# Low-part subtractions and mask additions on VectorE instead of GpSimd, in a one-layer conv and mLSTM kernel

## The chip, the cores and the metric

The kernel runs on one core of a Trainium2 chip. The metric is the device time of one execution in microseconds (us); the number given is the median of three runs. A profile is one execution recorded by the hardware, with its own span. Engine names in it: PE is TensorE (PEld its weight loads), DVE is VectorE, ACT is ScalarE, POOL is GpSimd, SP is SyncE, which here issues the DMAs.

## What is computed

One layer, applied to 128 context tokens and 2048 latent tokens of width 1024. The mixer joins a gated short convolution (512 channels) with a bidirectional mLSTM (4 heads of 128, chunks of 128 tokens); then comes a gated up projection with a convolution of width 3 over rows of the token grid, and a down projection. Everything is float32.

```python
def trunk_layer(x, mod, row_len, ffn_axis, C0, n0, m0, ...):
    shift1, scale1, gate1, shift2, scale2, gate2 = jnp.split(mod, 6, axis=-1)
    h = rmsnorm(x, norm1) * (1 + scale1) + shift1
    z = h @ w_in
    sc_b, sc_c, sc_x, q, k, v, o, g = jnp.split(z, idx, axis=-1)
    y_sc = sc_b * conv3(sc_c * sc_x, conv_sc_w, conv_sc_b)
    h_m, C, n, m = mlstm_bidir(q, k, v, gates(g), C0, n0, m0)   # chunked scans, forward and backward
    h_m = h_m * lax.rsqrt(jnp.mean(h_m * h_m, axis=-1, keepdims=True) + EPS) * mh_norm * jax.nn.sigmoid(o)
    x = x + gate1 * (jnp.concatenate([y_sc, h_m], axis=-1) @ w_out)
    h2 = rmsnorm(x, norm2) * (1 + scale2) + shift2
    a, gg = jnp.split(conv3(h2 @ w_up, conv_ffn_w, conv_ffn_b), 2, axis=-1)
    return x + gate2 * ((jax.nn.silu(gg) * a) @ w_down), C, n, m
```

Shapes, reshapes and biases are cut. `w_in` is 1024 x 3600, `w_up` 1024 x 5632, `w_down` 2816 x 1024. The outputs are the normed tokens of both groups and the final states of the context.

## The kernel before

**Products.** Each float32 product is three matmuls in a faster 32-bit format (fp32r): both operands are split into a high part (a copy rounded to that format, on ScalarE) and a low part (the operand minus its high part), and high·high, high·low and low·high are added in PSUM. So wherever a weight or an activation is loaded there is a ScalarE copy and a subtraction, and the subtraction of the low part is what the change moves. `load_w` (lines 101 to 109) splits the mixer's weights, 1024 columns at a time in two halves (line 108); `apply` (line 181) the normed tokens, every second block of 128 channels; `weights` (line 276) those of the up projection, `load_d` (line 993) those of the down projection in pieces of 704 columns.

**Stages.** The start (0 to about 130 us) prepares the modulation and the first normed tokens. To about 490 us come value and gate projections, the keys and the short convolution; to about 690 us the *Sums* weave, which carries the gated sums of keys and values over the chunks; to about 1020 us the *Mix* weave, which computes each chunk's output; to about 1180 us the output projection's rest and the sums of the normed tokens for the second half. The up projection (1180 to 2085) uses a Strassen–Winograd scheme: seven products per pair of blocks, whose combined operands come from `sums` (tokens, line 235) and `weights`. The down projection and the final norm end the run.

**The Mix weave.** A unit is a chunk and a pair of heads, 34 in all. `weave` runs them as a software pipeline: in one pass of its loop stand `first` of unit i, `third` of unit i−3, `second` of unit i−1, `load` of unit i+1, and a block of the projections' matmuls from `fill`, in every third pass a second one. So there are n + 4 = 38 passes.

- `load` fetches keys, queries, values and R, a broadcast read of 512 KB (line 742; three buffers).
- `first` multiplies keys and queries into S (line 753), adds the mask to R (line 754), takes exponentials on ScalarE (line 758), multiplies R with the queries into qs (line 761) and with S (line 762).
- `second` multiplies into y in PSUM (lines 773 and 775; one buffer), steps the state sf (line 779), and normalises: den (lines 783 to 785), then hv from y in two pairs of a ScalarE and a VectorE instruction (lines 790 and 791). The next unit's y can begin when the second line 791 has read the last.
- `third` transposes (line 803), scales into o2 (line 805) and stores it (line 808).

The blocks between them are `heads`, `shortconv` and `out_proj`; the last splits its tokens at lines 406 and 407 and adds squares at line 441.

**Order.** The kernel is written for a framework that places each instruction itself: from the text it builds a dependency graph, estimates what each instruction costs and when its inputs are there, and issues each engine's instructions in the order that follows. An engine then runs its queue strictly in order, and SP issues the DMAs in order too. An instruction given to another engine therefore also changes what stands before and behind it there.

Of the kernel before, what the change touches and what calls it, by code (L numbers as in the profile page):

```python
# [18 lines left out]
P = 128  # L19
# [26 lines left out]


def spans(t0, t1):
    """Token spans with the conditioning that they take."""
    return [(a, b, v) for a, b, v in ((t0, min(t1, P), 0), (max(t0, P), t1, 1)) if a < b]  # L50


# [1 line left out]
def hymba_kernel(ctx: ExitStack, tc: tile.TileContext, I, O):  # L54
# [46 lines left out]
    def load_w(src, n=1024):  # L101
        st = wp.tile([P, WN], F32, name="wst", bufs=2)
        Q.dma_start(st[:, :n], src)
        wh = wp.tile([P, WN], F32R, name="wh")
        S.activation(wh[:, :n], st[:, :n], AF.Copy)  # L105
        wl = wp.tile([P, WN], F32R, name="wl")
        for a in (0, n // 2):
            G.tensor_sub(wl[:, a:a + n // 2], st[:, a:a + n // 2], wh[:, a:a + n // 2].bitcast(F32))  # L108
        return wh, wl

    def affine(n, k0, k1):
# [2 lines left out]
                               bc(nrm[:, n, k0:k1, None], [P, k1 - k0, 2]), op0=ALU.add, op1=ALU.mult)  # L114

    def inv_rms(ss, n, r):
        """r [n tokens as columns of 128] = rsqrt(mean + eps) from the partial sums ss [P, n]."""
        nch = (n + P - 1) // P
        ps = pst.tile([P, 512], F32, name="st")
        for i in range(nch):  # L120
            w = min(P, n - i * P)
            PE.matmul(ps[:w, i:i + 1], ss[:, i * P:i * P + w], ones[:, 0:1], start=True, stop=True)
        for i0, i1, w in ((0, n // P, P), (n // P, nch, n % P)):
            if i0 < i1 and w:
                V.tensor_scalar(r[:w, i0:i1], ps[:w, i0:i1], 1.0 / D, EPS, op0=ALU.mult, op1=ALU.add)
                G.tensor_tensor(r[:w, i0:i1], r[:w, i0:i1], mhalf[:w, i0:i1], op=ALU.pow)  # L126

    def spread(r, n):
        """PSUM [P, n]: the columns of r along the free dimension, on every partition."""
        ps = pst.tile([P, 512], F32, name="st")  # L130
        for i in range((n + P - 1) // P):
            w = min(P, n - i * P)
            PE.matmul(ps[:, i * P:i * P + w], bc(r[:w, i:i + 1], [w, P]), ident[:w, :w], start=True, stop=True)  # L133
        return ps
# [27 lines left out]
    def apply(b, xt, norm):  # L162
        t0, n = BL[b]
        rb = spread(rcol(b), n)
        hH, hL = h_pair()
        sh = 0 if norm == 0 else 24
        for k in range(KT):
            x = xt[k // 4][:, k % 4]
            for a, e, v in spans(t0, t0 + n):
                a, e = a - t0, e - t0  # L170
                V.scalar_tensor_tensor(x[:, a:e], x[:, a:e], ab[:, norm, k, v:v + 1], rb[:, a:e],
                                       op0=ALU.mult, op1=ALU.mult)
                sv = modT[:, sh + k, v:v + 1]
                if k % 2 == 0:
                    S.activation(hH[:, k, a:e], x[:, a:e], AF.Identity, bias=sv)
                    V.scalar_tensor_tensor(hL[:, k, a:e], x[:, a:e], sv, hH[:, k, a:e].bitcast(F32),
                                           op0=ALU.add, op1=ALU.subtract)
                else:
                    S.activation(x[:, a:e], x[:, a:e], AF.Identity, bias=sv)
                    S.activation(hH[:, k, a:e], x[:, a:e], AF.Copy)  # L180
                    G.tensor_sub(hL[:, k, a:e], x[:, a:e], hH[:, k, a:e].bitcast(F32))
        return hH, hL

    def h_pair():
# [13 lines left out]
            PE.matmul(acc[:, :n], w_l, hH[:, k, :n], start=False, stop=(k == KT - 1))  # L198
        return acc

    # ------------------------------------------------------------- FFN
    # The up projection in seven products of half size (Strassen-Winograd): of the token blocks B11 B12
    # (first half of the features) and B21 B22, and of the weights' quarters A11 A12 (of a) and A21 A22 (of g).
    # A slot of the sums of tokens holds, for two pairs of blocks, 0: B12-B11, 1: B22-B12+B11, 2: B22-B12,
    # 3: B21-(1), 4: B21, 5: B22, 6: B11.
    ORDER = (6, 0, 1, 5, 2, 4, 3)

    def sums(hf, pool, pairs=range(2), direct=()):
        """The sums of the normed tokens of a half, to DRAM."""
        for p in pairs:  # L210
            t0 = hf * NU + 2 * NB * p
            rb = pool.tile([P, 2 * NB], F32, name="rb", bufs=1)
# [7 lines left out]
            for kk in range(4):  # L220
                f = pool.tile([P, 8 * NB], F32, name="F", bufs=2)
                xs_ = [(k, f[:, i * NB:(i + 2) * NB]) for i, k in ((4, kk + 4), (6, kk))]
                for k, x in xs_:
                    Q.dma_start(x, xD[k][:, t0:t0 + 2 * NB])
                yield
                for k, x in xs_:
                    for a, e, v in spans(t0, t0 + 2 * NB):
                        a, e = a - t0, e - t0
                        V.scalar_tensor_tensor(x[:, a:e], x[:, a:e], ab[:, 1, k, v:v + 1], rb[:, a:e],
                                               op0=ALU.mult, op1=ALU.mult)  # L230
                        S.activation(x[:, a:e], x[:, a:e], AF.Identity, bias=modT[:, 24 + k, v:v + 1])
                f = f.rearrange("p (i t) -> p i t", t=NB)
                V.tensor_sub(f[:, 0], f[:, 7], f[:, 6])
                V.tensor_sub(f[:, 1], f[:, 5], f[:, 0])
                G.tensor_sub(f[:, 2], f[:, 5], f[:, 7])
                V.tensor_sub(f[:, 3], f[:, 4], f[:, 1])
                for i in direct:
                    th, tl = slots[i]
                    S.activation(th[:, 4 * p + kk], f[:, i], AF.Copy)
                    V.tensor_sub(tl[:, 4 * p + kk], f[:, i], th[:, 4 * p + kk].bitcast(F32))  # L240
                yield
                i0, i1 = int(0 in direct), 7 - int(6 in direct)
                Q.dma_start(tD[hf, i0:i1, :, 4 * p + kk].rearrange("i p t -> p i t"), f[:, i0:i1])
# [14 lines left out]
            V.tensor_sub(tl[:, q], x, th[:, q].bitcast(F32))  # L258

    def weights(j):  # L260
        """The split weights of the seven products."""
        st = fp.tile([P, 2, 1024], F32, name="st", bufs=2)
        for m in range(2):
            Q.dma_start(st[:, m], I["w_up"][m * FT + j])
# [4 lines left out]
            op(t, a, b)  # L269
            return t  # L270

        def part(a, on_pool):
            wh = fp.tile([P, 512], F32R, name="wh", bufs=3)
            wl = fp.tile([P, 512], F32R, name="wl", bufs=3)
            S.activation(wh, a, AF.Copy)  # L275
            (G if on_pool else V).tensor_sub(wl, a, wh.bitcast(F32))  # L276
            return wh, wl

        yield part(a11, True)
        s1 = add(V.tensor_add, a21, a22, "s1")  # L280
        yield part(s1, False)
        s2 = add(V.tensor_sub, s1, a11, "s2")
        yield part(s2, False)
        s4 = add(V.tensor_sub, a12, s2, "s4")
        yield part(s4, False)
        s3 = add(V.tensor_sub, a11, a21, "s3")
        yield part(s3, False)
        yield part(a12, True)
        yield part(a22, True)

    def stages():
        """Products of all units, in order, each with its weights."""
        for hf in range(2):
            for j in range(FT):
                for i, w in enumerate(weights(j)):
                    yield hf, j, i, w

    # ---------------------------------------------------------------- mixer
    ph2 = ExitStack()
    with ExitStack() as ph1:  # L300
        wp = ph1.enter_context(tc.tile_pool(name="wp", bufs=4))
# [143 lines left out]
                else:  # L445
                    stats(grp, sss)

        # ---------------------------------------- second half of the tokens
        hs = {}
        with tc.tile_pool(name="start", bufs=1, side="right") as stp:  # L450
            def mod_pe(mt):
# [83 lines left out]

        ml = phr.enter_context(tc.tile_pool(name="ml", bufs=1, side="right"))

        # ------------------------------------------------------ gate rows
        WG, EM, AC = range(3)

        def row_scans(ls, ir, groups, m_in, dst):
# [139 lines left out]
            return v2  # L681

        class Sums:
            """The gated sums of a chunk's keys and values, both directions, for a pair of heads."""

            def __init__(self, c, hp):
                self.c, self.hp = c, hp
# [39 lines left out]
                pass  # L727

        class Mix:
            """The output of a chunk (-1: the context) for a pair of heads."""  # L730

            def __init__(self, c, hp):
                self.c, self.hp = c, hp
# [14 lines left out]
            def first(self):  # L748
# [2 lines left out]
                psS = pm.tile([P, 512], F32, name="S")  # L751
                for h in range(2):
                    PE.matmul(psS[:, h * P:(h + 1) * P], self.k2[:, h], self.q2[:, h], start=True, stop=True)
                G.tensor_add(W, W, bc(maskN[:, None], [P, 2, 2, P]))
                acol = colsel(self.cols, AC, max(c, 0), hp)
                for h in range(2):
                    for d in range(2):
# [50 lines left out]
                Q.dma_start(yD[4 + 2 * hp:6 + 2 * hp, :, t0:t0 + P].rearrange("h d t -> d h t"), o2)  # L808

        def weave(units, fill, extra):  # L810
            """Software pipeline: the stages of successive units between blocks of the projections."""
            n = len(units)
            for i in range(-1, n + 3):
                if 0 <= i < n:
# [8 lines left out]
                if extra and i % extra == 0:  # L823
                    next(fill, None)

        # ----------------------------------------- first half of the tokens
        run(vg(BA, hs, load_vg(0) + load_vg(1)))
        with tc.tile_pool(name="gt", bufs=1, side="right") as gt:
            gph = gate_phase()
# [128 lines left out]
                if not hf:  # L958
                    next(side, None)

    # the down projection and the final norm
    NG = 2 * NB
    with ExitStack() as ph3:
        dq = ph3.enter_context(tc.tile_pool(name="dq", bufs=2, side="right"))
# [18 lines left out]
        def load_d(m):  # L983
            ws = []
            n = FT * P // 2
            for q in range(2):
# [2 lines left out]
                wh = dq.tile([P, n], F32R, name="wh")  # L989
                wl = dq.tile([P, n], F32R, name="wl")  # L990
                S.activation(wh, st, AF.Copy)  # L991
                for e, a, b in ((G, 0, 704), (V, 704, n)):
                    e.tensor_sub(wl[:, a:b], st[:, a:b], wh[:, a:b].bitcast(F32))  # L993
                ws.append((wh, wl))
            return ws

# [142 lines left out]
```

## Time and profile before

| | before |
|---|---|
| median of 3 runs | 2623.24 us (2619.05 to 2626.44) |
| span of the profiled execution | 2622.1 us |
| PE busy | 2539.1 us (97%) |
| DVE busy | 1501.3 us (57%) |
| ACT busy | 1066.1 us (41%) |
| POOL busy | 706.4 us (27%) |
| DMA | 403.25 MB, 154 GB/s |
| mean granted TensorE clock | 0.988 |

For the profiled execution only its span is given, no time beside it; it is 1.1 us under the median. Engines run at once, so the shares don't add up; PE's is the one near the span. In rows of groups the columns are line, engine, operation, output and inputs with their shapes and count, then busy us and mean ns of one, then the idle time right before them and what ended it. In rows of waits they are engine, what waited, for what, then us in total, how often, and the longest. In rows of a timeline they are start, duration, engine, line, operation, tiles, count, and in brackets the idle time before.

### The profile page before, as it was taken

The page shows a single profiled execution, that of the slowest core. Times are in us where ns is not written, and L with a number is a line of the kernel's source. Part 1 is how long each engine was busy: PE and PEld are TensorE (multiplying, and loading weights), DVE is VectorE, ACT ScalarE, POOL GpSimd, SP SyncE. Part 2 cuts the span into 40 slices and gives each one's busy share as a digit, 9 for nine tenths or more (in the row PEclk, how much of TensorE's full clock was granted, in tenths as well). Part 3 has the DMA queues.
Part 4 walks back from the last instruction along what each step waited for, and adds up shares of the span by engine and source line. Part 5 has one row for each costly group of instructions (what it writes and reads, how often), then busy time and mean ns, then how long its engine had stood idle before and what let it go on. Part 6 is the DMA issues. An engine that isn't in the chain of part 4 may idle for free. (4 is left out here: it accounts for less than half of the span.)

```text
span 2622.1 us, 46918 instructions
## 1 busy us (share of the span) xinstructions
PE 2539.1 (97%) x18511; PEld 2519.2 (96%) x18511; DVE 1501.3 (57%) x2560; ACT 1066.1 (41%) x2028; POOL 706.4 (27%) x534
## 2 busy tenths in 40 slices
PE   8999999999988988899999999999999999999998
PEld 7999999999988988899999999999999999999998
DVE  3993242333457666797686669666666635353533
ACT  4521142322345454464454446554544523232411
POOL 2542242211333344221121112111111222232232
PEclk9999999999999999999999999999999999999999
DMA  8773142555467887854252224222222635454442
GB/s 280 250 254 101 57 140 85 155 180 155 152 195 242 253 256 235 267 195 139 84 178 91 79 79 165 83 83 82 83 83 90 234 113 184 156 179 150 149 139 77
DMA packets 223582, 403.25 MB, mean 154 GB/s; under 512 B 20722, under 2 KB 144770, under 8 KB 221698
## 3 DMA queue, kind: packets, MB, share of 16 engines
q1 hardware_dynamic: 223362, 400.25, 46.5%
q8 instruction: 145, 2.38, 0.4%
q14 instruction: 75, 0.61, 0.1%
HBM read 305.13 MB, written 95.04 MB: 153 GB/s over the span
## 5 line engine op out<-in xcount | busy, mean ns | idle before, releaser
L196 PE MATMUL acc<-hH,wh 128*128 128x384 f32 (+1 forms) x1536 | 516.4, 336 | 0.0
L198 PE MATMUL acc<-hH,wl 128*128 128x384 f32 (+1 forms) x1536 | 505.0, 329 | 0.0
L197 PE MATMUL acc<-hL,wh 128*128 128x384 f32 (+1 forms) x1536 | 504.7, 329 | 0.0
L938 PE MATMUL pa<-tH,wh 128*128 128x272 f32 x1408 | 410.1, 291 | 5.6 <-DVE raw L950 5.2
L940 PE MATMUL pa<-tH,wl 128*128 128x272 f32 x1408 | 409.3, 291 | 0.4 <-DVE wl L276 0.4
L1030 PE MATMUL d<-uh,wh 128*128 128x272 f32 x1408 | 406.0, 288 | 3.1 <-ACT raw L948 3.1
L939 PE MATMUL pa<-tL,wh 128*128 128x272 f32 x1408 | 407.1, 289 | 0.0
L1032 PE MATMUL d<-uh,wl 128*128 128x272 f32 x1408 | 406.9, 289 | 0.0
L1031 PE MATMUL d<-ul,wh 128*128 128x272 f32 x1408 | 404.4, 287 | 0.0
L276 POOL TENSOR_TENSOR wl<-st,wh 128x512 fp32r<-128x512 f32 x132 | 182.3, 1381 | 730.5 <-ACT wh L275 697.5
L108 POOL TENSOR_TENSOR wl<-wst,wh 128x512 fp32r<-128x512 f32 (+1 forms) x160 | 234.3, 1486 | 434.0 <-ACT wh L105 421.5
L196 PEld LDWEIGHTS acc<-hH,wh 128*128 128x128 f32 x1536 | 291.1, 190 | 1.5 <-issue 0.4
L197 PEld LDWEIGHTS acc<-hL,wh 128*128 128x128 f32 x1536 | 291.1, 189 | 1.0
L198 PEld LDWEIGHTS acc<-hH,wl 128*128 128x128 f32 x1536 | 290.5, 189 | 0.2 <-issue 0.2
L938 PEld LDWEIGHTS pa<-tH,wh 128*128 128x128 f32 x1408 | 266.8, 190 | 6.4 <-issue 5.7
L1030 PEld LDWEIGHTS d<-uh,wh 128*128 128x128 f32 x1408 | 266.9, 190 | 3.4 <-ACT raw L948 3.3
L939 PEld LDWEIGHTS pa<-tL,wh 128*128 128x128 f32 x1408 | 267.3, 190 | 0.0
L940 PEld LDWEIGHTS pa<-tH,wl 128*128 128x128 f32 x1408 | 266.6, 189 | 0.6 <-DVE wl L276 0.6
L1032 PEld LDWEIGHTS d<-uh,wl 128*128 128x128 f32 x1408 | 266.1, 189 | 0.1
L1031 PEld LDWEIGHTS d<-ul,wh 128*128 128x128 f32 x1408 | 265.3, 188 | 0.0
L993 POOL TENSOR_TENSOR wl<-st,wh 128x704 fp32r<-128x704 f32 x64 | 150.5, 2352 | 367.2 <-ACT wh L991 358.2
L884 DVE SCALAR_TENSOR_TENSOR tt<-raw,fw,tt 128x127 f32<-128x127 f32 (+4 forms) x264 | 245.7, 959 | 1.5 <-ACT tt L890 0.8
(215 smaller groups left out, 5031.6 us busy)
## 6 DMA issues: line engine op xcount, KB each, us to landing
st<-in_w_up SPq DMA_DIRECT2D x88, 512.0 KB, 4.4
st<-in_w_down SPq DMA_DIRECT2D x64, 704.0 KB, 4.2
wst<-in_w_in SPq DMA_DIRECT2D x48, 512.0 KB, 4.1
us<-uD SPq DMA_DIRECT2D x88, 272.0 KB, 4.4
R<-nD SPq DMA_DIRECT2D x34, 512.0 KB, 5.5
wm<-in_w_modr SPq DMA_DIRECT2D x32, 512.0 KB, 4.7
F<-tD SPq DMA_DIRECT2D x12, 1088.0 KB, 8.8
uD<-tt SPq DMA_DIRECT2D x22, 576.0 KB, 2.8
```

Of the source, the lines that this page charges most:

```text
L108: G.tensor_sub(wl[:, a:a + n // 2], st[:, a:a + n // 2], wh[:, a:a + n // 2].bitcast(F32))
L196: PE.matmul(acc[:, :n], w_h, hH[:, k, :n], start=(k == 0), stop=False)
L197: PE.matmul(acc[:, :n], w_h, hL[:, k, :n], start=False, stop=False)
L198: PE.matmul(acc[:, :n], w_l, hH[:, k, :n], start=False, stop=(k == KT - 1))
L276: (G if on_pool else V).tensor_sub(wl, a, wh.bitcast(F32))
L884: V.scalar_tensor_tensor(o, i, w, o, op0=ALU.mult, op1=ALU.add)
L938: PE.matmul(acc, wh[:, w], rh, start=(kk == 0 and i in (0, 1, 5)), stop=False, skip_group_check=True)
L939: PE.matmul(acc, wh[:, w], rl, start=False, stop=False, skip_group_check=True)
L940: PE.matmul(acc, wl[:, w], rh, start=False, stop=(kk == 3), skip_group_check=True)
L1030: PE.matmul(acc[b][:, :NB], wh[:, c], uh[:, q], start=(j == 0), stop=False)
L1031: PE.matmul(acc[b][:, :NB], wh[:, c], ul[:, q], start=False, stop=False)
L1032: PE.matmul(acc[b][:, :NB], wl[:, c], uh[:, q], start=False, stop=(j == FT - 1))
```

## The change

Every low-part subtraction that GpSimd did, and the mask's addition, is issued to VectorE. On GpSimd remain the powers of lines 126 and 795 and a memset. The rest of the diff blanks comments and is left out; line numbers are the same in both.

```diff
 def load_w(src, n=1024):                                   # 160 instructions
         for a in (0, n // 2):
-            G.tensor_sub(wl[:, a:a + n // 2], st[:, a:a + n // 2], wh[:, a:a + n // 2].bitcast(F32))
+            V.tensor_sub(wl[:, a:a + n // 2], st[:, a:a + n // 2], wh[:, a:a + n // 2].bitcast(F32))
 def apply(b, xt, norm):                                    # 32
-                    G.tensor_sub(hL[:, k, a:e], x[:, a:e], hH[:, k, a:e].bitcast(F32))
+                    V.tensor_sub(hL[:, k, a:e], x[:, a:e], hH[:, k, a:e].bitcast(F32))
 def sums(hf, pool, pairs=range(2), direct=()):             # 16
-                G.tensor_sub(f[:, 2], f[:, 5], f[:, 7])
+                V.tensor_sub(f[:, 2], f[:, 5], f[:, 7])
 def weights(j):                                            # 132: a11, a12, a22
-        def part(a, on_pool):
+        def part(a):
-            (G if on_pool else V).tensor_sub(wl, a, wh.bitcast(F32))
+            V.tensor_sub(wl, a, wh.bitcast(F32))
 class Mix, first(self):                                    # 34
-                G.tensor_add(W, W, bc(maskN[:, None], [P, 2, 2, P]))
+                V.tensor_add(W, W, bc(maskN[:, None], [P, 2, 2, P]))
 def load_d(m):                                             # 64
-                for e, a, b in ((G, 0, 704), (V, 704, n)):
-                    e.tensor_sub(wl[:, a:b], st[:, a:b], wh[:, a:b].bitcast(F32))
+                for a, b in ((0, 704), (704, n)):
+                    V.tensor_sub(wl[:, a:b], st[:, a:b], wh[:, a:b].bitcast(F32))
```

Two places show how the order moves. The first is VectorE's queue in the second half of the Mix weave, from one unit's line 762 to the next line 791 and a little on. Before:

```order
L762 TENSOR_TENSOR R<-S,R 128x2x256
L805 SCALAR_TENSOR_TENSOR o_8101<-st,mhn,o_8101 128x128 x2
L779 SCALAR_TENSOR_TENSOR sf_4844<-sf_4844,decB,sb 128x129 x2
L783 TENSOR_TENSOR den<-y,cols 128x4
L761 TENSOR_TENSOR qs<-R,q_8408 128x512
L784 SCALAR_TENSOR_TENSOR den<-y,den 128x4
L407 TENSOR_TENSOR hL<-xt,hH 128x384
L785 RECIPROCAL den<-den 128x4
L791 SCALAR_TENSOR_TENSOR hv<-y,den,hv 128x128 x2
L794 TENSOR_SCALAR hss<-hss 128x2
```

And now:

```order
L805 SCALAR_TENSOR_TENSOR o_8101<-st,mhn,o_8101 128x128 x2
L779 SCALAR_TENSOR_TENSOR sf_4844<-sf_4844,decB,sb 128x129 x2
L783 TENSOR_TENSOR den<-y,cols 128x4
L754 TENSOR_TENSOR R<-R,maskN 128x2x256
L784 SCALAR_TENSOR_TENSOR den<-y,den 128x4
L761 TENSOR_TENSOR qs<-R,q_8408 128x512
L785 RECIPROCAL den<-den 128x4
L108 TENSOR_TENSOR wl<-wst,wh 128x512
L791 SCALAR_TENSOR_TENSOR hv<-y,den,hv 128x128
L108 TENSOR_TENSOR wl<-wst,wh 128x512
L407 TENSOR_TENSOR hL<-xt,hH 128x384
L791 SCALAR_TENSOR_TENSOR hv<-y,den,hv 128x128
```

Two subtractions of line 108 and an addition of line 754 have come in between the first line 783 and the second line 791; in other passes line 754 stands right behind the second line 791 and ahead of line 762. SP's queue has the load of R (line 742) right behind the store of line 808 in most passes, before and now; here as it is now:

```order
L808 DMA yD<-o_7648 128x2x128
L742 DMA R<-nD 128x1024
L680 DMA v_8046<-vD 128x258
L675 DMA o_7930<-oD 128x2x128
L675 DMA q_8048<-qD 128x2x128
L746 DMA sb<-sD 128x516
```

Nothing moved there; what changed is that the engine which uses R first is now the one whose line 805 the store waits for. The second place is VectorE's queue in the second half of the up projection, where the pair of additions of line 950 ends each of the products. Before:

```order
L276 TENSOR_TENSOR wl<-s_21317,wh 128x512
L269 TENSOR_TENSOR s_21564<-st 128x512
L905 TENSOR_TENSOR tt<-tt 128x1152
L950 TENSOR_TENSOR raw_21243<-pb,c_21335 128x272
L950 TENSOR_TENSOR raw_21243<-pb,c_21349 128x272
L950 TENSOR_TENSOR raw_21244<-pa,c_21299 128x272
L950 TENSOR_TENSOR raw_21244<-pa,c_21314 128x272
L950 TENSOR_TENSOR raw_21243<-pc,c_21260 128x272
```

And now:

```order
L905 TENSOR_TENSOR tt<-tt 128x1152
L276 TENSOR_TENSOR wl<-st,wh 128x512
L950 TENSOR_TENSOR raw_21243<-pb,c_21335 128x272
L950 TENSOR_TENSOR raw_21243<-pb,c_21349 128x272
L276 TENSOR_TENSOR wl<-st,wh 128x512
L950 TENSOR_TENSOR raw_21244<-pa,c_21299 128x272
L950 TENSOR_TENSOR raw_21244<-pa,c_21314 128x272
L276 TENSOR_TENSOR wl<-st,wh 128x512
L950 TENSOR_TENSOR raw_21243<-pc,c_21260 128x272
```

Each pair of line 950 has one more subtraction (a11, a12 or a22 of a weight block) in front of it.

More of the change, by code (lines that the diff above doesn't have):

```diff
@@ L275, in part @@
             S.activation(wh, a, AF.Copy)
-            (G if on_pool else V).tensor_sub(wl, a, wh.bitcast(F32))
+            V.tensor_sub(wl, a, wh.bitcast(F32))
             return wh, wl
-        yield part(a11, True)
+        yield part(a11)
         s1 = add(V.tensor_add, a21, a22, "s1")
-        yield part(s1, False)
+        yield part(s1)
         s2 = add(V.tensor_sub, s1, a11, "s2")
-        yield part(s2, False)
+        yield part(s2)
         s4 = add(V.tensor_sub, a12, s2, "s4")
-        yield part(s4, False)
+        yield part(s4)
         s3 = add(V.tensor_sub, a11, a21, "s3")
-        yield part(s3, False)
-        yield part(a12, True)
-        yield part(a22, True)
+        yield part(s3)
+        yield part(a12)
+        yield part(a22)
     def stages():
```

## Prediction

> **What bounds the kernel now.** I read the page's head first, then the busy time by stage (columns: stretch, its length, then busy us and instruction count of PE, weight loads, VectorE, ScalarE and GpSimd, then granted clock, DMA share, GB/s). The stages are the start, the Mix weave, its end with the second half's sums, the up projection and the down projection.
>
> ```profile
> span 2622.1 us, 46918 instructions
> PE 2539.1 (97%) x18511; PEld 2519.2 (96%) x18511; DVE 1501.3 (57%) x2560; ACT 1066.1 (41%) x2028; POOL 706.4 (27%) x534
> ...
> 0.00:131.00 131.00, 118.08 (x888) 116.64 (x889) 86.63 (x175) 61.40 (x121) 51.41 (x60) 0.99 0.79 265
> 131.00:490.00 359.00, 355.64 (x2324) 352.31 (x2323) 154.72 (x306) 99.06 (x186) 107.47 (x93) 0.99 0.41 128
> 490.00:690.00 200.00, 199.43 (x1134) 194.12 (x1133) 63.39 (x118) 53.66 (x122) 36.75 (x26) 1.00 0.54 162
> 690.00:1020.00 330.00, 296.30 (x1890) 292.68 (x1889) 204.16 (x526) 166.26 (x499) 127.25 (x111) 0.96 0.73 229
> 1020.00:1180.00 160.00, 149.94 (x1039) 148.31 (x1038) 125.84 (x203) 82.99 (x149) 50.23 (x41) 0.96 0.70 234
> 1180.00:2085.00 905.00, 895.03 (x7057) 893.57 (x7056) 649.31 (x927) 462.08 (x791) 177.34 (x130) 0.99 0.31 108
> 2085.00:2622.00 537.00, 524.65 (x4192) 521.58 (x4191) 217.21 (x308) 140.66 (x160) 155.97 (x77) 0.99 0.44 147
> ```
>
> TensorE is busy in 2539.1 of 2622.1 us, so everything that VectorE and GpSimd do can be worth 83 us at most, and 33.7 of these (330 − 296.3) lie in the Mix weave, the only long stretch with PE well under full and a granted clock of 0.96. Next I asked what PE waits for.
>
> ```profile
> PE y L773 <- DVE hv L791: 33.3, 14, 6.9
> PE st L122 <- DVE ss L441: 8.3, 3, 6.5
> ...
> PE pa L938 <- DVE raw L950: 5.2, 3, 1.9
> PE st L133 <- POOL fr L126: 3.9, 8, 1.0
> ...
> PE acc L335 <- POOL hL L181: 2.2, 1, 2.2
> ...
> PE acc L334 <- POOL wl L108: 1.0, 1, 1.0
> ...
> PE pc L940 <- POOL wl L276: 0.9, 1, 0.9
> ```
>
> The three rows at the end that name a moved instruction (hL, wl, wl) hold 4.1 us together. GpSimd's lateness therefore costs PE almost nothing; what the change can alter is VectorE, for which PE waits 33.3 us at line 791 of the Mix weave.
>
> **The prices.**
>
> ```profile
> L276 POOL TENSOR_TENSOR wl<-st,wh 128x512 fp32r<-128x512 f32 x132 | 182.3, 1381 | 730.5 <-ACT wh L275 697.5
> L108 POOL TENSOR_TENSOR wl<-wst,wh 128x512 fp32r<-128x512 f32 (+1 forms) x160 | 234.3, 1486 | 434.0 <-ACT wh L105 421.5
> L993 POOL TENSOR_TENSOR wl<-st,wh 128x704 fp32r<-128x704 f32 x64 | 150.5, 2352 | 367.2 <-ACT wh L991 358.2
> L754 POOL TENSOR_TENSOR R<-R,maskN 128x512 f32<-128x512 f32 x34 | 46.0, 1354 | 116.5 <-DMA R<-nD 114.5 <-PE st L803 1.9
> L276 DVE TENSOR_TENSOR wl<-s,wh 128x512 fp32r<-128x512 f32 x176 | 120.7, 686 | 8.4 <-ACT wh L275 8.4
> L993 DVE TENSOR_TENSOR wl<-st,wh 128x704 fp32r<-128x704 f32 x64 | 59.0, 921 | 137.4 <-ACT wh L991 136.8 <-DMA us<-uD 0.5
> L1046 DVE TENSOR_TENSOR ss<-ss,sq 128x544 f32<-128x544 f32 x27 | 55.7, 2062 | 0.0
> L980 DVE TENSOR_TENSOR ul<-us,uh 128x544 fp32r<-128x544 f32 x88 | 68.3, 829 | 3.9 <-ACT uh L979 3.9
> ```
>
> A 512-wide subtraction takes 1381 to 1486 ns on GpSimd and 686 ns on VectorE, a 704-wide one 2352 against 921. VectorE gets about 132·0.69 + 160·0.69 + 34·0.69 + 64·0.92 = 283 us, and with the 48 narrower ones of lines 181 and 235 about 310. In return its instructions no longer stretch while GpSimd runs: line 1046 takes 2062 ns where line 980, same width, takes 829. That is the lock, and the Mix weave shows it at its sharpest:
>
> ```profile
> 817.87 2.81 POOL L108 TENSOR_TENSOR wl<-wst,wh 128x512 fp32r<-128x512 f32 x2 [2.63 <-ACT wh L105]
> ...
> 819.74 2.88 DVE L407 TENSOR_TENSOR hL<-xt,hH 128x384 fp32r<-128x384 f32 x2
> ...
> 820.64 1.57 POOL L754 TENSOR_TENSOR R<-R,maskN 128x512 f32<-128x512 f32 x1
> ...
> 822.81 0.54 DVE L407 TENSOR_TENSOR hL<-xt,hH 128x384 fp32r<-128x384 f32 x1
> ...
> 823.03 0.77 PE L773 MATMUL y<-sf,qs 128*128 128x129 f32 x2 [4.74 <-DVE hv L791]
> ```
>
> Two of line 407's subtractions take 2.88 us beside GpSimd, one takes 0.54 alone; line 791 stands behind them, and PE waits 4.74 us. [...] The trace bears out the kind of stall and not that sum: I took, for each VectorE instruction, its excess over the shortest of its form, and this is 188 us over the whole span, 34.6 of them in the Mix weave. So 310 us come to VectorE and 188 go: it gets about 120 us fuller, 57% to 62% of the span. That it stays far under full says nothing by itself, since only places where PE waits for it count.
>
> **The change by stages.** The profiled execution is 1.1 us under the median of the runs (2623.24); I sum against its 2622.1.
>
> *Start, 0 to 131.* The 2.2 us that PE waits for hL of line 181 go: on VectorE, which is at the bias of the next token block then, the subtraction takes half the time. Bounds −2.2 and +2 (line 108's subtractions stand ahead of other work of VectorE there). I take −2.2.
>
> *131 to 690.* PE is busy 555 of 559 us and VectorE 218. Weights are prepared well ahead, the cover is VectorE's idle 61%. Zero, bounds −1 and +3.
>
> *Mix weave, 690 to 1020.* 44 subtractions of line 108 and 31 of line 754 come to VectorE, 75·0.686 = 51.5 us, and 34.6 are given back: 17 us more. Where they stand matters more than their sum. The new order puts line 108 between lines 783, 784, 785 and 791, the chain for which PE waits, and line 754 ahead of line 762, or even between the two of line 791. In the case above VectorE would lose the 1.8 us of stretch on line 407 and gain two of line 108 and one of line 754, 2.1 us, in the same chain: an exchange, no gain. PE waits for line 791 in 14 of the 38 passes of the loop (34 units and the filling and emptying of the pipeline); elsewhere its projection matmuls cover VectorE. 17·14/38 = +6.3 us. Bounds: −16 when the two longest lock cases and their dip of the clock vanish without anything in their place (the rivals), +17 when all of it lands on the path.
>
> Line 754 adds a wait as well: it needs R, a transfer, and on GpSimd it held back nothing but GpSimd.
>
> ```profile
> POOL R L754 <- DMA R<-nD: 100.1, 21, 10.4
> ...
> R<-nD SPq DMA_DIRECT2D x34, 512.0 KB, 5.5
> ...
> 764.41 0.47 PE L773 MATMUL y<-sf,qs 128*128 128x129 f32 x2 [3.55 <-DVE hv L791]
> ...
> 769.62 0.69 DVE L761 TENSOR_TENSOR qs<-R,q 128x512 f32<-128x512 f32 x1 [2.62 <-DMA R<-nD]
> 769.68 1.79 POOL L754 TENSOR_TENSOR R<-R,maskN 128x512 f32<-128x512 f32 x1 [5.99 <-DMA R<-nD]
> ...
> 823.97 0.68 DVE L762 TENSOR_TENSOR R<-S,R 128x512 f32<-128x512 f32 x1
> ...
> 824.57 0.60 DVE L805 SCALAR_TENSOR_TENSOR o<-st,mhn,o 128x128 f32<-128x128 f32 x2
> ...
> 826.59 0.33 SPq L742 DMA_DIRECT2D R<-nD  x1
> ```
>
> In VectorE's queue lines 762, 805, 779, 761 and 783 of older units stand behind it, and PE waits for what they give. Worse, SP issues the load of R (line 742) behind the store of line 808, which waits for line 805 on VectorE. So a ring closes: line 805 (0.60), 1.42 us until SP has issued line 742, 5.5 to its landing, line 754 (0.69), line 762 (0.68), the next line 805: 8.9 us a round, against 330/38 = 8.7 a pass today. Where VectorE reaches line 754's new place before R's landing of the trace of before (13 units), the gaps add up to 31 us; it is nothing when the passes leave room. The nearest row is the one landing that VectorE already waits for (2.62 us, line 761 at 769.62), beside the 3.55 us that PE lost in that unit. I take one more such loss, +3.5, and keep 0 and +31.
>
> *1020 to 1180.* VectorE is at 79%. About 22 us come (32 subtractions of 0.69) and 20.9 of stretch go. Zero, bounds ±5: PE's 6.5 us for line 441 fall in this stage, and a subtraction of line 108 ahead of that line would lengthen them as much as an end of the stretch shortens them.
>
> *Up projection.* Three subtractions in seven products go to VectorE. Their place is ahead of line 950's additions, where VectorE idles:
>
> ```profile
> DVE raw L950 <- PE pa L940: 74.4, 73, 1.1
> ```
>
> About 1.0 us of waiting for PE ahead of each holds 0.69 us. Line 276's sums come to 123·0.69 = 84 us for 905, beside 30 returned; 649 busy becomes 703 of 905. Cover if that is wrong: three buffers of wl. Zero, bounds −4 (the waits for lines 950 and 276) and +6.
>
> *Down projection.* 64·0.92 = 59 us against 47 of stretch, 36.5 of it on line 1046; VectorE is at 40%. PE's 3.9 us for fr stay, since line 126 stays on GpSimd. Zero, ±2.
>
> Sum: 2622.1 − 2.2 + 6.3 + 3.5 = 2629.7, and 1.1 more for the median: **2631**.
>
> **The rivals.** *The locks pay* (faster). The two longest waits of PE behind stretched instructions vanish (the 4.74 us above and the longest of the row, 6.9, at 933), with the dips of the granted clock that follow:
>
> ```profile
> 930.00:960.00 30.00, 27.15 (x164) 26.89 (x165) 19.55 (x58) 17.31 (x52) 12.23 (x12) 0.85 0.78 241
> ```
>
> 30 us at 0.85 are 4.5 us of clock. −11.6 − 4.5 − 2.2 gives 2604 (2605 by the median), and the rest of the 33.3 us could add as much again in part. For it speaks that these are the two longest waits of the weave; against it that the new instructions stand in the same chain. It decides when line 108 falls beside the matmul blocks and not into the chain.
>
> *The exchange is hidden* (same): VectorE's extra 17 us fall where PE has cover; 2622 to 2624. [...] The 24 passes without a wait speak for it, the 14 with one against.
>
> *The ring binds* (slower). 8.7 us is the mean of passes that are not equal: every third one carries a second block of projection matmuls, and the others, which are shorter, would be drawn out to the ring's length. Two thirds of the 31 us are then on PE's path, +21, and with the 6.3 us of the exchange and some clock the time is 2650. For it speaks that in the first half of the weave line 754 stands in the same pass as the line 805 that releases its load; against it that a long pass gives VectorE room for the two short ones. It decides as soon as a short pass finds VectorE without a lead of some 2 us over PE.
>
> **How the numbers follow.** A difference under 0.3% (7.9 us) is about what cannot be told from none. My forecast has 0.45 and its own range of 2622 to 2642; a third of it lies under 0.3%. The locks pay 0.24, hidden 0.18, the ring 0.13. Faster is 0.24; same 0.18 + 0.14 = 0.32; slower 0.31 + 0.13 = 0.44. The range from 2607 to 2655 leaves out the full payment of the locks and a ring on every pass.
>
> **What would show it.** Right: line 407 at 0.55 and line 779 at 0.35 us everywhere; VectorE near 1620 us and GpSimd near 60; PE's wait for line 791 at 40 us or more, with waits of VectorE for R at line 754; the stages from 1180 on at 905 and 537 us. Wrong: the wait for line 791 under 20 us (locks), or a new long row of line 754 waiting for R with PE's Mix stage over 350 us (the ring), or an up projection over 911 us, where line 276 would then stand in front of line 950.

## The result and the profile after

The changed kernel takes 2587.68 us (median of 4 runs, 2581.26 to 2600.82) where the one before takes 2624.65; the ratio is 0.9875, with a 95% interval of 0.9846 to 0.9905. Run again beside other kernels it gave 2585.56 and a ratio of 0.9873 (0.9858 to 0.9888). By the medians it is 37 us faster, by the ratio 33; 8 us slower had been forecast, and the time lies under the stated range of 2607 to 2655. The profiled execution took 2581.26 us, 6 less than the median; it is the fastest of the four, and the gains by stage below are taken from it.

The head of the page of the changed kernel, to be set against the two lines shown of before:

```profile
span 2579.5 us, 46461 instructions
...
PE 2524.3 (98%) x18511; PEld 2505.3 (97%) x18511; DVE 1602.7 (62%) x2994; ACT 1069.5 (41%) x2028; POOL 53.8 (2%) x100
```

VectorE is at 1602.7 us, near the 1620 of the prediction, and GpSimd at 53.8. What was not expected stands under PE: the same 18511 matmuls keep it busy for 2524.3 us and not 2539.1. So the 42.6 us between the two profiled spans are 27.8 us less of PE's idle time (83.0 to 55.2) and 14.8 us less of busy time for the same work.

Where they arise, by the start of the first or last matmul of a line in the two traces (us):

| up to | before | after | gain in the stage |
|---|---|---|---|
| first gate projection (line 333) | 40.45 | 42.90 | −2.4 |
| first unit of Mix (line 753) | 688.25 | 678.84 | 11.9 |
| last unit of Mix (line 775) | 1010.43 | 988.02 | 13.0 |
| first up product (line 938) | 1114.02 | 1083.94 | 7.7 |
| first down product (line 1030) | 2066.13 | 2024.42 | 11.6 |
| end of PE's work | 2615.23 | 2572.64 | 0.9 |

By its first product the up projection begins at 1114 us, and not at 1180 as the stages above have it. One profile's stages also differ by some us for no reason of the change: with line 276 or line 993 alone on VectorE (below), neither of which runs in the Mix weave, the weave takes 2.7 and 3.0 us longer than before.

The busy time of the Mix weave, the stage behind it and the up projection, cut at these marks, first before, then after (columns as in the prediction):

```profile
688.00:1010.00 322.00, 288.30 (x1843) 284.76 (x1842) 199.07 (x512) 162.25 (x488) 122.74 (x108) 0.96 0.74 230
1010.00:1114.00 104.00, 94.66 (x605) 93.39 (x604) 72.89 (x135) 44.69 (x92) 35.65 (x29) 0.96 0.78 252
1114.00:2066.00 952.00, 941.44 (x7421) 939.54 (x7421) 692.79 (x992) 494.09 (x846) 194.72 (x143) 0.99 0.32 111
```

```profile
679.00:988.00 309.00, 284.62 (x1843) 281.65 (x1843) 212.13 (x589) 163.70 (x489) 27.59 (x35) 0.98 0.78 240
988.00:1084.00 96.00, 93.73 (x602) 92.48 (x600) 70.17 (x156) 43.50 (x91) 2.64 (x3) 0.98 0.83 263
1084.00:2024.00 940.00, 937.45 (x7420) 935.61 (x7420) 759.16 (x1133) 496.60 (x845) 1.55 (x2) 1.00 0.32 113
```

In the weave VectorE has 13 us more to do (199 to 212; 17 were forecast) in 13 us less time. In the up projection it has 66 more, and PE's idle time falls from 10.6 to 2.6 us. PE's waits after:

```profile
PE y L773 <- DVE hv L791: 22.8, 12, 3.7
...
PE st L133 <- POOL fr L126: 4.0, 8, 1.1
...
PE st L122 <- DVE ss L1046: 1.7, 1, 1.7
```

The wait for line 791 went from 33.3 to 22.8 us and its longest from 6.9 to 3.7 (18.4 and 3.8 in a second profile of the changed kernel); the waits for lines 441 (8.3) and 950 (5.2) are gone from the list. VectorE's forms after:

```profile
L108 DVE TENSOR_TENSOR wl<-wst,wh 128x512 fp32r<-128x512 f32 x144 | 96.0, 684 | 71.6 <-ACT wh L105 71.4
...
L407 DVE TENSOR_TENSOR hL<-xt,hH 128x384 fp32r<-128x384 f32 x40 | 21.3, 549 | 9.4 <-ACT hH L406 9.3
...
L1046 DVE TENSOR_TENSOR ss<-ss,sq 128x544 f32<-128x544 f32 x27 | 19.4, 718 | 0.7 <-ACT sq L1045 0.7
L779 DVE SCALAR_TENSOR_TENSOR sf<-sf,decB,sb 128x129 f32<-128x129 f32 x60 | 18.6, 346 | 0.1
```

Line 1046 takes 718 ns where it took 2062, line 407 549 where it took 632 on average, line 779 346 for 527: the stretches are gone.

### The profile page after: what moved, and what is told of

The parts are those of the page before. It is cut to its first block, busy times and chain, and to the rows that moved or that the text cites. A ratio compares the mean times of both kernels' runs of the same rounds, so it can differ in the third digit from the quotient of the medians.

```text
span 2579.5 us, 46461 instructions
## 1 busy us (share of the span) xinstructions
PE 2524.3 (98%) x18511; PEld 2505.3 (97%) x18511; DVE 1602.7 (62%) x2994; ACT 1069.5 (41%) x2028; POOL 53.8 (2%) x100
## 4 chain that ended last, share of the span: by engine, by line
PE 83%; DMA 8%; DVE 5%; ACT 2%; issue 1%; SPq 1%; POOL 1%; DVEq 0%; ACTq 0%; POOLq 0%
PE acc L196 8%; PE acc L198 8%; PE acc L197 8%; PE pa L938 6%; PE pa L940 6%; PE pa L939 6%; PE d L1032 6%; PE d L1030 6%; PE d L1031 6%; PE pb L940 3%; PE pb L938 3%; PE pb L939 3%; PE pc L939 2%; PE pc L940 2%; PE pc L938 2%
## 5 line engine op out<-in xcount | busy, mean ns | idle before, releaser
L991 ACT ACTIVATE wh<-st 128x1408 fp32r<-128x1408 f32 x64 | 88.3, 1379 | 354.1 <-PE d L1031 200.6
L940 PE MATMUL pb<-tH,wl 128*128 128x272 f32 x704 | 203.7, 290 | 0.2 <-DVE wl L276 0.2
L938 PE MATMUL pb<-tH,wh 128*128 128x272 f32 x704 | 203.5, 289 | 0.0
```

The lines of the kernel that those rows point to most:

```text
L938: PE.matmul(acc, wh[:, w], rh, start=(kk == 0 and i in (0, 1, 5)), stop=False, skip_group_check=True)
L940: PE.matmul(acc, wl[:, w], rh, start=False, stop=(kk == 3), skip_group_check=True)
```

## The experiments

Theories: the *lock* (VectorE's instructions are stretched while GpSimd reads SBUF, as line 1046 with 2062 ns before and 718 after; ending that is the gain), *late parts* (the low parts came too late from a slow engine), *order* (the queues' new order helps), and from the prediction the *exchange* and the *ring*.

**The lock put back, by reads and by writes.** All the work stays on VectorE; GpSimd gets work that nobody needs.

```diff
 # lockR: behind V.tensor_sub at lines 108, 276 (a11, a12, a22) and 993
+            G.tensor_sub(st[...], st[...], wh[...].bitcast(F32))
 # lockW: at the same places
+            [G.memset(st[...], 0.0) for _ in range(3)]
```

> The changed kernel with GpSimd instructions that nobody needs: behind VectorE's low-part subtractions of lines 108, 276 (parts a11, a12, a22) and 993, GpSimd subtracts too, in place in the loaded weights, whose contents are dead by then (160, 132 and 64 instructions, the sizes GpSimd had before). All work stays on VectorE. Lock theory (what the change gains is that VectorE's instructions with two SBUF inputs no longer stand still while GpSimd reads SBUF): the stretches come back, line 1046 over 1.3 us a piece, PE's wait for line 791 over 30 us, and the time is 2615 to 2650. Late-part theory (the low parts simply came too late from the slower engine): they still come early, 2583 to 2597. Order theory (the new order of the queues is what helps): 2583 to 2600.

> As the run before it, but in place of each subtraction three memsets of GpSimd over the same piece of the dead weights: GpSimd is busy at the same places, holds the same buffers and writes SBUF, but reads none of it. Lock theory in its narrow form (only a GpSimd instruction that reads SBUF shuts VectorE out): no form of VectorE is stretched, 2580 to 2600. Wide form (any GpSimd instruction does): line 1046 over 1.3 us, 2610 to 2640. Late-part and order theories: 2583 to 2600.

Measured: 2666.1 us with the reads, ratio to before 1.0181 (1.0158 to 1.0205), and 2586.0 with the writes, 0.9869 (0.9849 to 0.9888). First two groups of VectorE and one of GpSimd with the reads, then two with the writes (added lines shift the numbers: 1052 is line 1046, 278 is 276):

```profile
L278 DVE TENSOR_TENSOR wl<-st,wh 128x512 fp32r<-128x512 f32 x132 | 135.7, 1028 | 1.8
...
L1052 DVE TENSOR_TENSOR ss<-ss,sq 128x544 f32<-128x544 f32 x27 | 56.0, 2075 | 0.7 <-ACT sq L1051 0.7
```

```profile
L110 POOL TENSOR_TENSOR wst<-wst,wh 128x512 f32<-128x512 f32 x144 | 220.4, 1542 | 518.4 <-issue 273.7 <-DVE wl L108 194.1 <-DVE den L790 39.3
```

```profile
L1052 DVE TENSOR_TENSOR ss<-ss,sq 128x544 f32<-128x544 f32 x27 | 19.4, 717 | 0.0
```

```profile
L110 POOL MEMSET wst<- 128x512 f32 x432 | 217.5, 527 | 503.3 <-DVE wl L108 484.2 <-issue 4.5 <-ACT hv L795 4.1
```

GpSimd works about as long in both (220 and 217 us at line 110). Reading, it stretches line 1046 to 2075 ns and takes back the whole gain and 45 us more; writing, it costs nothing. Late parts and order predicted about 2590 for both and fall with the reads: the low parts come from VectorE in both. The reads cost more than expected (2615 to 2650), and the moved subtractions are stretched too (1028 ns for 690). PE's wait for line 791 did not come back over 30 us, as the lock theory had it, but to 25.1; 30.7 us of the loss against before fall between the first up and the first down product, where line 950 is the longest of several waits of PE:

```profile
PE pa L943 <- DVE raw L955: 8.7, 7, 2.7
```

(lines 938 and 950). That loss is not shown to be the stretch alone, because in this stage the two runs differ in one thing more. The reading subtractions all need ScalarE's copy of a22, the memsets don't, and VectorE waits longer for the next weights, first with the reads, then with the writes (line 271 is line 269):

```profile
DVE s L271 <- DMA st<-in_w_up: 124.4, 36, 5.1
```

```profile
DVE s L271 <- DMA st<-in_w_up: 17.3, 18, 2.2
```

What that wait costs PE was not separated from the stretch. In the Mix weave no wait of VectorE is longer like that with the reads, and there they take back 11.2 of the 13.0 us: 320.4 us between the marks, and 309.2 with the writes as in the changed kernel.

Not every form is stretched. Lines 1046 and 276 have both inputs in SBUF; line 950, which has one in PSUM, takes 429 to 434 ns on average with the reads and 439 to 440 with the writes, and line 791, which reads y from PSUM, 348 and 349.

**One move at a time.** Each is the kernel before with one line on VectorE, here line 108:

```diff
-            G.tensor_sub(wl[:, a:a + n // 2], st[:, a:a + n // 2], wh[:, a:a + n // 2].bitcast(F32))
+            V.tensor_sub(wl[:, a:a + n // 2], st[:, a:a + n // 2], wh[:, a:a + n // 2].bitcast(F32))
```

> The kernel before with line 108 alone moved to VectorE. Lock theory: line 108 is 234 of the some 372 us that GpSimd works before the up projection, and the change gained 30 us there, so 15 to 24 us of gain, 2600 to 2609, all before the up projection begins; PE's wait for line 791 under 28. Exchange theory of the prediction (line 108 puts back into VectorE's chain what the lock took out): 2620 to 2632.

> The kernel before with line 276's parts a11, a12, a22 alone moved to VectorE. The change gained 11.6 us between the first and the last product of the up projection, where the prediction had put zero. Lock theory: this move alone brings it, 8 to 14 us of gain, all in the up projection, 2607 to 2614, and the stages before it stay where they were. If it came from the earlier stages (tokens' sums ready sooner, since lines 235 and 108 had gone): 2617 to 2624.

> The kernel before with the mask's addition, line 754, alone moved to VectorE. Ring theory (line 754 makes VectorE wait for R, with the work of older units behind it): slower by 3 to 20 us, 2624 to 2641, PE's wait for line 791 over 36 us. Lock theory: 34 reading instructions of 1.35 us less beside VectorE's chain, 2 to 10 us of gain, 2612 to 2620.

> The kernel before with line 993's 64 subtractions alone moved to VectorE. They gave VectorE back more than they put on it (line 1046 goes from 2.06 to 0.72 us a piece, 36 us, for 59 us of new work), yet the down projection ended only 0.9 us earlier in the changed kernel: all theories expect no change, 2616 to 2626. Over 5 us either way would mean that the order set by line 993 reaches back into the up projection.

| moved alone | median | ratio (95%) | gain |
|---|---|---|---|
| line 108 | 2602.13 | 0.9933 (0.9914 to 0.9952) | 19.4 of 2621.48 |
| line 276 | 2612.39 | 0.9958 (0.9941 to 0.9974) | 9.4 of 2621.82 |
| line 754 | 2619.21 | 0.9991 (0.9980 to 1.0001) | 2.6 of 2621.82, not told from none |
| line 993 | 2618.12 | 0.9978 (0.9968 to 0.9987) | 3.7 of 2621.82 |

Together 35.1 us, where the change gained 37.0 and 33.9 in its two comparisons (by the ratios 37, and 33 for the change): the parts add up within the scatter of the runs. The 48 narrower subtractions of lines 181 and 235 were not moved alone. Line 108 alone gains 10.5 us between the marks of the Mix weave, 9.4 between the first gate projection and the first unit of Mix and 6.2 in the stage behind the weave, and it loses 4.8 in the up projection. Line 276 alone gains 10.5 between the first up and the first down product, as the lock theory said; ahead of the up projection it gains nothing in sum. The exchange's forecast for line 108 fell, and the ring's for line 754. With line 754 alone, the profile's waits of VectorE and of PE are:

```profile
DVE R L754 <- DMA R<-nD: 22.6, 19, 3.7
```

```profile
PE y L773 <- DVE hv L791: 28.5, 15, 5.5
```

VectorE does stand before line 754 for R, 22.6 us, as the ring had it (and once 8.4 us before the weave begins); and yet PE waits less for line 791 than before (33.3). The hold and the 34 reads less come to 2.6 us, the low end of what the lock theory gave, and not told from none. The mirror of it, line 754 alone left on GpSimd:

```diff
-                V.tensor_add(W, W, bc(maskN[:, None], [P, 2, 2, P]))
+                G.tensor_add(W, W, bc(maskN[:, None], [P, 2, 2, P]))
```

> The changed kernel with line 754, the mask's addition, back on GpSimd; all else on VectorE. In the changed kernel VectorE stands 34 us before line 754 for R. Ring theory of the prediction (line 754 holds back the work queued behind it on VectorE, though the rest of the change gains more): faster than the changed kernel by 4 to 12 us, 2576 to 2584. Lock theory: 34 reading instructions of 1.35 us in the Mix weave stretch VectorE's chain again, and the hold cost nothing: slower by 3 to 12, 2590 to 2600.

2592.5 us, 0.9892 (0.9868 to 0.9915): slower than the changed kernel as the lock theory had it, if at all, for the intervals overlap.

**Twice the work of line 108 on VectorE.**

```diff
+            for _ in range(2):
-            V.tensor_sub(wl[:, a:a + n // 2], ...)
+                V.tensor_sub(wl[:, a:a + n // 2], ...)
```

> The changed kernel with each subtraction of line 108 done twice on VectorE, 160 more of 0.69 us (110 us), 44 of them in the Mix weave. Exchange theory of the prediction (what line 108 puts on VectorE lands on PE's path in the share of passes in which PE waits): 44 times 0.69 us by 14 of 38 passes are +11 in the weave, with some more in the stage behind it, so 10 to 25 us over the changed kernel, 2597 to 2612. Filling theory (the subtractions run where VectorE waits for ScalarE's line 790, a wait that fell from 45.4 to 18.9 us in the changed kernel, and where PE has cover): at most 8 over, 2583 to 2595, the wait for line 790 lower again.

2594.9 us, 0.9900 (0.9883 to 0.9916), 9.3 over the changed kernel beside it. The sum sits between the two forecasts; the stages tell them apart. Between the marks of the Mix weave, where 42 extra instructions are 27 us, the time rises by 1.3 us (307.7 to 309.0), not by 11. 6.1 us of loss fall in the stage behind it and 5.9 between the first gate projection and the first product of the Sums weave; the stages without line 108 differ by −3.7 (up) and +2.4 us (down). PE's wait for line 791 in this run, 18.4 us in the changed kernel beside it (774 and 792 are lines 773 and 791):

```profile
PE y L774 <- DVE hv L792: 19.8, 12, 4.9
```

The other sign of the filling theory did not come: VectorE's wait for line 790 is not lower again, 21.9 us for 20.1 beside it. In the weave the extra work went elsewhere, into VectorE's waits before lines 441, 407 and 754, which fall from 9.7, 9.2 and 26.9 us to 0.2, 1.6 and 18.8, 25 us in sum.

**Two attempts on the wait for R.** One issues the store of line 808 from GpSimd, so that the load of R is not behind it on SP; the other loads R a pass earlier, into four buffers.

```diff
 # store_pool
-                Q.dma_start(yD[4 + 2 * hp:6 + 2 * hp, :, t0:t0 + P]..., o2)
+                G.dma_start(yD[4 + 2 * hp:6 + 2 * hp, :, t0:t0 + P]..., o2)
 # r4, in weave (load_r holds the DMA of R that load had)
+                for k in ((0, 1) if i < 0 else (i + 2,)):
+                    if k < n:
+                        units[k].load_r()
```

> The changed kernel with the store of line 808 issued by GpSimd, which now has room, in place of SP: the load of R (line 742) no longer stands behind a store that waits for VectorE's line 805. In the changed kernel VectorE waits 34 us for R before line 754 and PE 22.8 us for line 791. Ring theory: the wait for R falls under 12 us, PE's wait for line 791 under 17, and the time by 4 to 10, 2576 to 2583. If the ring costs nothing (VectorE runs far enough ahead of PE): the wait for R falls and the time does not, 2583 to 2592. [...]

> The changed kernel with R loaded a pass earlier, into four buffers in place of three (and one buffer in place of two for ScalarE's scratch tile sj). Ring theory: VectorE's 34 us before line 754 fall under 10, PE's wait for line 791 under 17, and with it go half-clock stretches of the Mix weave: 6 to 16 us under the changed kernel, 2570 to 2582. If VectorE has the room anyway: the wait for R falls and the time stays within 4 us.

> The changed kernel again, beside the two runs after it on the same chip: 2580 to 2595 by every theory.

The first is slower than the changed kernel, 2601.3 us, 0.9919 (0.9905 to 0.9934), with a longer wait for R; most of the loss is in the Mix weave, 324.4 us between its marks for 309.2; the second is the same, 2584.3, 0.9864 (0.9848 to 0.9880), and its wait for R did not fall under 10. The waits, first of the one, then of the other (lines 754 and 760 are the mask's addition):

```profile
DVE R L754 <- DMA R<-nD: 38.2, 24, 5.2
```

```profile
DVE R L760 <- DMA R<-nD: 28.0, 19, 3.2
```

So neither removed what it was to remove. The first lies over both forecasts (2576 to 2592), and the store lands 4.0 us after its issue and not 2.8 (medians), but whether that, the wait for R or the half-clock stretches (in which the granted clock is 0.50) come first was not separated. What the ring costs in the changed kernel stays open; without the hold, with line 754 on GpSimd, the time was not shorter (2592.5 us).

## Why the prediction was wrong

**The exchange, "17·14/38 = +6.3 us", is the step that failed**, in sign: the weave gained 13.0 us. Of the 50 us between the span forecast (2629.7) and the measured one (2579.5), 23 lie in the weave, whose forecast was +9.8 with the ring's 3.5. The exchange's sum was near (13 us more on VectorE, 17 forecast). What failed is the view that line 108 between lines 783 and 791 lengthens that chain. VectorE stands idle in the chain, for ScalarE's line 790. That wait, before and after:

```profile
DVE hv L791 <- ACT hv L790: 45.4, 55, 3.6
```

```profile
DVE hv L791 <- ACT hv L790: 18.9, 32, 0.8
```

26.5 of the 45.4 us are gone from it, and with line 108 alone moved 15.7 are (29.7 left). The doubled line 108 cost 1.3 us in the weave, though not by way of this wait. So the subtractions went mostly into idle time of VectorE, the first of them in part into this wait; that it is why the chain did not grow longer is argued from these figures. The stretches, in contrast, fell on work that stood ahead of line 791, as on line 407's pair; line 791 itself took 337 to 353 ns in all 68 cases before and 341 to 352 after. The place that the prediction showed with a wait of 4.74 us, in the changed kernel:

```profile
799.17 0.68 DVE L108 TENSOR_TENSOR wl<-wst,wh 128x512 fp32r<-128x512 f32 x1
...
800.51 0.68 DVE L108 TENSOR_TENSOR wl<-wst,wh 128x512 fp32r<-128x512 f32 x1
...
801.31 1.03 DVE L407 TENSOR_TENSOR hL<-xt,hH 128x384 fp32r<-128x384 f32 x2
...
802.39 0.35 DVE L791 SCALAR_TENSOR_TENSOR hv<-y,den,hv 128x128 f32<-128x128 f32 x1
802.66 1.02 DVE L407 TENSOR_TENSOR hL<-xt,hH 128x384 fp32r<-128x384 f32 x2
...
803.60 0.34 DVE L791 SCALAR_TENSOR_TENSOR hv<-y,den,hv 128x128 f32<-128x128 f32 x1
804.09 0.46 PE L773 MATMUL y<-sf,qs 128*128 128x129 f32 x2 [1.40 <-DVE hv L791]
```

Two of line 108 do stand in the chain, but the pair of line 407 between the two of line 791 takes 1.02 us where it took 2.88, and PE waits 1.40 us.

**"83 us at most" left out the clock.** The gain stayed under it, but it counted PE's idle time and not the half-clock stretches that follow it. These are stretches of the kernel before, cut where the granted clock changes, and a wait that stands right ahead of the first:

```profile
874.00:877.40 3.40, 3.40 (x18) 3.40 (x17) 3.01 (x7) 3.19 (x8) 3.09 (x3) 0.50 0.43 136
928.60:938.80 10.20, 5.98 (x24) 6.01 (x25) 7.08 (x20) 4.72 (x15) 4.91 (x5) 0.50 0.69 202
1109.50:1119.70 10.20, 6.96 (x31) 6.99 (x32) 6.42 (x11) 3.58 (x7) 0.85 (x1) 0.50 0.86 309
```

```profile
873.68 0.52 PE L773 MATMUL y<-sf,qs 128*128 128x129 f32 x2 [2.01 <-DVE hv L791]
```

The records of the clock have 12 such stretches before, apart from one that begins with the last matmuls, 58 us together, and 6 after, 20.5 us; at half speed that is 29 and 10 us of lost clock, 19 less. PE was busy in 49.3 us of the stretches before and in 20.1 of those after; half of that is 24.7 and 10.0 us, and the difference, 14.6, is nearly all of the 14.8 us by which PE's busy time fell. Nine of the 12 are 3.41 us long, one is 6.83 and two are 10.24; the 6 after are 3.41 each. In 11 of the 12 and in all 6 an idle time of PE of 1.4 to 6.9 us ends in the stretch or at most 3.2 us ahead of it; the one that begins at 478.0 us has none over 0.3 us in the 13 us ahead. The wait of 2.01 us shown above stood ahead of a stretch; another, of 2.47 us before 988.32, had none behind it, so the length of a wait alone did not decide.

**The stages put at zero** were not. 131 to 690, bounded by −1 and +3, gave 7.9 us: PE's 555 busy us of 559 hid two half-clock stretches, which are gone. Not all of this is the change's, since with line 276 or line 993 alone, neither of which runs there, PE also reaches the first unit of Mix 1.9 and 3.6 us sooner than before; with line 108 alone it is 8.8. The up projection, bounded by −4, gave 11.6, 10.5 by line 276 alone, with which the wait for line 950 (5.2 us) and the stretch behind it go; the wait for line 948 (3.1) is 2.5 us then and 0.7 with the whole change. Its cover argument was right as to the 66 us of new work, which cost nothing; the term missed what the lock had cost there. 1020 to 1180 gave 7.7 (between the marks at 1010 and 1114), with the wait for line 441 (6.5 and a stretch of 10.24 us) gone.

The start was forecast at −2.2. The first gate projection begins 2.4 us later, but the wait for hL stood behind its first matmul, at 45.68, and is gone: the matmul that began at 131.1 us begins at 129.6. With other lines moved it begins at 129.9 to 131.5, so this term is neither borne out nor refuted.

**Right** were the prices (line 108 at 684 ns, line 754 at 687), VectorE's sum within some 20 us, the wait for fr (4.0 for 3.9), the down projection (0.9 us), and the ring's hold itself, 26.2 us of waiting for R in the changed kernel (34 with one wait of 8.0 before the weave begins). The sign that PE's wait for line 791 would be 40 us or more did not come. That this hold would cost PE 3.5 us was not borne out: line 754 alone made nothing slower. The rival *the locks pay* gave 2604 for the Mix weave's two longest waits and their dip; it had the mechanism and only a part of the places.

## What to carry to other kernels

Where VectorE and GpSimd both read SBUF, as in this kernel (line 1046 at 2062 ns beside GpSimd's subtractions, 718 without), price a GpSimd instruction not by its own time but by what it stretches on VectorE, and look for such stretches by comparing a form's mean with its shortest, in every stage and not only in the one with the largest waits. Work added to a queue was cheap here where its engine already waited for another (42 more subtractions, 27 us, cost 1.3 us in the weave); the stretches lengthened what stood ahead of the critical instruction (line 407's pair, 2.88 us before and 1.02 after), and TensorE's wait behind it (4.74 and 1.40 us). Count a wait of TensorE together with the half-clock stretch that the records show behind it; in this kernel that made the gain half as large again (14.8 us beside 27.8). And when a second experiment puts work back, look for what else it changes, as the wait for the weights did here.

## What was not expected of the hardware

GpSimd busy with 217 us of memsets at line 108's place, and 630 us in all, changed nothing (2586.0 us): it is the reading subtractions that stretch VectorE's instructions (line 1046 at 2075 ns, 717 with the memsets). With both engines doing the subtractions the time is 80 us longer (2666.1), more than the change had gained, and VectorE's busy time grows from 1604.8 to 1773.5 us; how much of the 80 us is the stretch and how much the later weights stays open.
